# Expert weights loaded in rows of 8 KB, with the mixers' buffers in halves of the same places

## The chip, the cores and the metric

One core of one Trainium2 chip. The time is that of one execution on the device, in microseconds (us): the median of 3 runs. The engines are TensorE (PE, with its weight loads as PEld), VectorE (DVE), ScalarE (ACT), GpSimd (POOL) and SyncE (SP); sixteen DMA engines move data between the memory of the chip and the core's own, and work beside them.

## What is computed

One layer of a hybrid decoder for 512 tokens of width 1024, in f32. Four token mixers share one input projection; a layer norm follows, then 32 experts of which each token uses four, then an embedding with a gate, and a second layer norm.

```python
u = x @ w_in                                   # columns of SSD, RWKV-7, GLA, mLSTM
mix = concat([ssd(u_a), rwkv7(u_b), gla(u_c), mlstm(u_d)]) @ w_out
x = layer_norm(alpha * x + mix)
top_val, top_idx = top_k(x @ router_w + router_b, 4)
gate = softmax(top_val)
# for each token t and each of its four experts e:
hg, hl = split(x[t] @ w_gu[e] + b_gu[e], 2)    # 1024 x 2048
hg = minimum(hg, 7.0); hl = clip(hl, -7.0, 7.0)
y = ((hl + 1.0) * hg * sigmoid(1.702 * hg)) @ w_down[e] + b_down[e]
ffn[t] += gate[t, e] * y
h = alpha * x + ffn
h = h + sigmoid(h @ ple_gate_w) * (p @ ple_proj)
out = layer_norm(h)
```

Each expert has 12 MB of weights, 384 MB in all, and all of them are read once.

## The kernel before

**Stages.** The mixers, the output projection, the first layer norm and the router run from 0 to about 402 us. The 32 experts run one after the other from there to about 1496 us, and the end (the gate of the embedding, the second norm, the stores) to 1576.

**One expert.** The experts are sorted by the number of their tokens (`listed`, L1147), so that 18 get three groups of 32 · 4 slots each and 14 get two; `TURN` mixes them, and the first two in turn are the experts 0 and 1 themselves. In the loop at the end, `up` (L1293) multiplies the tokens' columns with the gate and value weights, 8 steps of k in four column quarters for each group; `swiglu` follows on DVE and ACT; `turned` transposes with TensorE; `tokens` (L1279) transposes the next expert's gathered rows; `down` (L1308) makes the second product; `put` scales and adds the rows in memory (`accd`) with a scatter from POOL (L1327). `dispatch` with `picked` (L1091) finds tokens and gates of the expert two places ahead with small matmuls, and `load` (L1208) gathers the next expert's rows of x from memory (`x1d`) into one of two `xg` buffers. For the first expert, `ranked`, `gates` and three dispatches stand between its up and its down product, then the gather for expert 1, and `blocks` (L1362), which makes a table of slots that did not fit.

**The weights' ring.** An expert's weights are 24 pieces of 128 x 1024 numbers, 512 KB, a row of 4 KB for each of 128 partitions. They are loaded by SP into a ring of 32 places (`seq`, L876) and, in the first round, into 4 more (`pp`), in the order of use. Most places are tiles that the mixers used before: 14 of tag `rb`, 8 of `r2`, 8 of `r3`, 2 of `wr`. `ahead` loads the first 15 pieces during the output projection. `unit` (L1213) issues one load when the piece that held the place before is marked `used`, that is after its last matmul in program order; `pump` issues as many as are free. Each load waits on SP for the place, and for a load eight issues before it. From the third expert on, the number of the expert is read from the sorted list `eii` by SP (`values_load`, L1228) once for each expert, at its first load in program order. The scheduler that builds the kernel sets the order of instructions on an engine; from the first expert on, TensorE keeps program order.

**At expert 20** three pieces more are loaded, the tokens' embeddings and their projection (`embed`); at the end, eight pieces of the gate's weights.

**In the mixers** two things matter here. Tiles of tag `rb` are what the change moves: `G` (products of the RWKV chain), `Tt` and `AQ` (its triangular inverse), `rk`, `ep`, `kp` and others. The chain has eight chunks in order; in each, a copy of the product `WO` to `W` (L445) waits for TensorE and TensorE's next step waits for it. `pj` and `pt` are products of the input projection, which fill TensorE between the chain's steps.

Of the kernel before, what the change touches and what calls it, by code (L numbers as in the profile page):

```python
# [8 lines left out]
F32 = mybir.dt.float32  # L9
# [16 lines left out]

SLOTS = {"rb": 14, "xh": 8, "wr": 2, "wh": 2, "wl": 2, "zb": 4, "zc": 7, "yy": 2, "rc": 4, "rd": 6, "mc": 5, "md": 4}
BANKS = {"r": 2, "o": 1, "p": 2, "m": 3}
RING2 = 8
RING3, XG, AB = 8, 2, 2  # L30
NS = 3
# [4 lines left out]
GROUPS_OF = [NS if r < BIG else NS - 1 for r in range(32)]  # L36
OPT = {"conv": ("sx0",), "lnt": ("vv","va","aa","va"), "lov": ("zb",), "pl": (0,5,8,13,16,21), "pt": (), "em": 20, "wk": 6, "ml": 0, "hold": 0, "gm": (0,), "pe": 0, "order": "SABZDIgvLqmoM", "wm": (10,8,0), "bn": (), "ad": (), "rb": (2,0,3), "pf": {(0,1):15}, "ex": 4, "xq": 1, "aq": 1,  "ap": 2, "t1": (8,8), "pa": 1,  "op": ((2,1),(0,))}
EMPTY = 4096.0
# [88 lines left out]
def mixers(tc, nc, A, rbp, dram, mix, ctx, ident, ones, tri, x1d, accd, R, dbg):  # L127
# [7 lines left out]
    pg = mix.enter_context(tc.tile_pool(name="pg", bufs=1, space=PSUM))  # L135

    def tl(tag, shape, name, dtype=F32):
        return {"rb": rbp, "zb": wz, "zc": wz, "rd": wz, "wr": wrp, "yy": wq, "rc": wq, "mc": wq}.get(tag, wk).tile(shape, dtype, name=name, tag=tag, bufs=SLOTS[tag])

# [141 lines left out]
    def rwkv():  # L281
# [596 lines left out]
    room = {**SLOTS, "r2": RING2, "r3": RING3, "pp": NT}  # L878

    def raw(look=False):  # L880

        n = R["n"]
        if n < len(seq) + OPT["ex"]:
            tag = (seq[:-2] + ["pp"] * OPT["ex"] + seq[-2:])[n]
        else:
            tag = seq[(n - OPT["ex"]) % len(seq)]
        if look:
            return tag, R["at"].get(tag, 0) % room[tag]
        R["n"] += 1
        R["at"][tag] = R["at"].get(tag, 0) + 1  # L890
        return R["pools"][tag].tile([128, D], F32, name="w", tag=tag, bufs=room[tag])

    def ahead(n):

        for _ in range(n):
            R["taken"].append(raw(look=True))
            w = raw()
            sy.dma_start(w, A["we"][0, len(R["pre"])])
            R["pre"].append(w)
# [159 lines left out]
def moe(ctx, tc, nc, A, ident, rbp, R, x1d, accd, ovt, ove, out, dbg):  # L1059
# [3 lines left out]
    xg = [xp.tile([128, D], F32, name=f"xg{i}", tag=f"xg{i}") for i in range(XG)]  # L1063
    g.memset(xg[0], 0.0)
    ep = ctx.enter_context(tc.tile_pool(name="ep", bufs=1))
# [58 lines left out]
    def gateweights():  # L1124

        for k in range(KT):
            w = ring[len(srcs) - KT + k]
            pool, tag, n = [(R["pools"]["r3"], "r3", RING3), (R["pools"]["wr"], "wr", SLOTS["wr"])][k] if k < 2 else (rbp, "rb", SLOTS["rb"])
            hi, lo = (pool.tile([128, D], F32R, name=x, tag=tag, bufs=n) for x in ("wh", "wl"))
# [71 lines left out]
    def dispatch(e):  # L1201

        picked(e, onehots(e, dp), lambda i: R["aux"][:, i, e], 5, e > 0, True)

# [10 lines left out]
    def unit(tag_of, src):  # L1215
# [9 lines left out]
        if isinstance(src, tuple):  # L1225
            j, u = src
            if j not in place:
                place[j] = nc.values_load(eii[0:1, TURN[j]:TURN[j] + 1], engines=[mybir.EngineType.SP], min_val=0, max_val=E - 1)  # L1228
            sy.dma_start(w[:, None], A["we"][bass.ds(place[j], 1), u].rearrange("o p n -> p o n"))
        else:  # L1230
            sy.dma_start(w, src)
        waits[tag, n] = len(ring)
# [4 lines left out]
    for e in range(E):  # L1237
        if e == OPT["em"]:
            srcs += [A["pT"], A["pproj"][0], A["pproj"][1]]
        srcs += [A["we"][e, u] if e < 2 else (e, u) for u in range(24)]  # L1240
    srcs += [A["pgw"][k] for k in range(KT)]
    base = lambda e: 24 * e + (3 if e >= OPT["em"] else 0)
    npre = len(R["pre"])
# [49 lines left out]
    def up(p, e, xT, g_, ks, last):  # L1293
        for k in ks:
            for c in range(4):
                w = ring[base(e) + 2 * k + c // 2][:, 512 * (c % 2):512 * (c % 2) + 512]
                ordered(pe.matmul(p[32 * c:32 * c + 32], xT[:, k, g_:32 * GROUPS_OF[TURN[e]]:GROUPS_OF[TURN[e]]], w,  # L1297
                                  start=False, stop=(k == KT - 1), tile_position=(0, 32 * c)))
            if last:
                used(base(e) + 2 * k)  # L1300
                used(base(e) + 2 * k + 1)

    def down(p, e, hT, ks, last):
        m = None
        for k in ks:
            for c in range(4):
                w = ring[base(e) + 16 + k][:, 256 * c:256 * c + 256]
# [38 lines left out]
    def embed(i, tag):  # L1346

        at = base(OPT["em"]) - 3
        pT, *pw = ring[at:at + 3]
        ppt.append(tp.tile([128, D], F32, name=f"pp{i}", tag="pp", bufs=NT))  # L1350
        tk = slice(128 * i, 128 * i + 128)
        for h in range(2):
            p = bank(tag, "emb")
            n = slice(512 * h, 512 * h + 512)
            for k in range(2):
                ordered(pe.matmul(p, pT[:, 512 * k:512 * k + 512][:, tk], pw[k][:, n], start=(k == 0), stop=(k == 1)))
            s.activation(ppt[i][:, n], p, AF.Copy)
        if i == NT - 1:
            for i in range(3):
                used(at + i)  # L1360
# [37 lines left out]
    def overflow(then):  # L1398
        with tc.tile_pool(name="ov", bufs=1) as ov:
            n = nc.values_load(tot[0:1, 0:1], min_val=0, max_val=24)  # L1400
            with tc.For_i(0, n, 1) as j:
# [24 lines left out]
                v.tensor_add(d[:, 3:4], d[:, 2:3], d[:, 3:4])  # L1426
                v.tensor_add(d[:, 3:4], d[:, 3:4], d[:, 4:5])
                def big(name):
                    return ring2.tile([128, D], F32, name=name, tag="r2", bufs=RING2)

# [16 lines left out]
                def product(ps, xT, units, view, o):  # L1447
                    for k in range(KT):
                        wt = big("wt")
                        sy.dma_start(wt[:, None], A["we"][bass.ds(e, 1), units[k]].rearrange("o p n -> p o n"))  # L1450
                        for i in range(2):
# [35 lines left out]
    with tc.issue_after(ix0), tc.issue_after(ld0):  # L1487
        g.dma_start(accd, x1d)
        for t in xg[1:]:
            g.memset(t, 0.0)  # L1490
        listed()
    for j in range(E):
# [30 lines left out]
        hT.extend(turned(act[:ns - 1], ["h"] * (ns - 1)))  # L1523
        if more and j:
            nxt = tokens(j + 1)
        hT.extend(turned(act[ns - 1:], ["h"]))
        pd = []
        for g_ in range(ns):
            pd.append(opened(j, "dn", 2048, 256))
            down(pd[g_], j, hT[g_], range(3), g_ == ns - 1)  # L1530
        for k in range(3, KT):
            for g_ in range(ns):
                down(pd[g_], j, hT[g_], [k], g_ == ns - 1)
        if j == OPT["em"]:
            embed(3, "gu")
        if more and not j:
            nxt = tokens(j + 1)
        for g_ in range(ns):
# [7 lines left out]
    def transposed(src):  # L1546

        hi, lo = (r3.tile([128, KT, 128], F32R, name="h" + x, tag="r3", bufs=RING3) for x in "hl")
        for h in range(2):
# [19 lines left out]
    def finish():  # L1569
        hs = []  # L1570
        for i in range(NT):
            hs.append(ring2.tile([128, D], F32, name=f"h{i}", tag="r2", bufs=RING2))
            for n in (slice(0, 512), slice(512, D)):
# [52 lines left out]
def _lay_out(inp, experts=True):  # L1626
# [45 lines left out]
    bg = a["exp_b_gu"][0].reshape(E, 2, 4, 256).transpose(0, 2, 1, 3).reshape(E, 2 * D)  # L1672
    r["bias"] = np.concatenate([bg, a["exp_b_down"][0]], 1)
    if experts:
        gu = a["exp_w_gu"][0].reshape(E, KT, 128, 2, 2, 2, 256).transpose(0, 1, 4, 2, 5, 3, 6).reshape(E, 16, 128, D)
        r["we"] = np.concatenate([gu, a["exp_w_down"][0].reshape(E, KT, 128, D)], 1)
    r["pT"] = a["p"][0, 0].T.reshape(2, 128, T).transpose(1, 0, 2).reshape(128, 2 * T)
    r["pproj"] = a["ple_proj"][0].reshape(2, 128, D)
    r["pgw"] = a["ple_gate_w"][0].reshape(KT, 128, D)
    return {k: np.ascontiguousarray(v) for k, v in r.items()}  # L1680
# [23 lines left out]
```

## Time and profile before

| | |
|---|---|
| median of 3 runs | 1579.39 us (1577.28 to 1581.19) |
| the profiled execution | 1578.24 us, of it the span from first to last instruction 1576.4 |
| TensorE busy | 1462.9 us (93%), weight loads 776.0 |
| VectorE, ScalarE, GpSimd busy | 522.9, 301.7, 218.2 us |
| moved by DMA | 466.13 MB, mean 296 GB/s |
| granted TensorE clock | 0.961 in the mean |

The profile is of one execution on the core. An engine counts as busy while it has an instruction, also when that instruction holds on for data. A share of the DMA engines is that of sixteen; it can be a little over 1, since packets of two queues overlap in the records. A number of microseconds after "<-" in a view is idle time and what ended it.

### The profile page before, as it was taken

What the parts mean: (1) busy time and instruction counts of PE and PEld (TensorE: products, weight loads), DVE (VectorE), ACT (ScalarE), POOL (GpSimd) and SP (SyncE); (2) the same over time, 40 slices, a digit from 0 to 9 for tenths busy, and PEclk for the clock granted to TensorE, in tenths of its full rate; (3) what the DMA queues carried; (4) which work ended last, traced back from release to release, by engine and by line L of the source; (5) the groups of instructions that cost most, each with busy time, mean ns of one, the idle gap of its engine ahead of it and who ended that gap; (6) DMA issues with size and microseconds to landing.
All of it is one profiled execution on the core that took longest, in us unless ns stands there. A gap on an engine that the chain in (4) does not pass through costs nothing. (4 is left out here: it accounts for less than half of the span.)

```text
span 1576.4 us, 36036 instructions
## 1 busy us (share of the span) xinstructions
PE 1462.9 (93%) x14672; PEld 776.0 (49%) x14672; DVE 522.9 (33%) x1597; ACT 301.7 (19%) x632; POOL 218.2 (14%) x222
## 2 busy tenths in 40 slices
PE   9989999997799999999999999999999998999985
PEld 5769879886244433443334333334434343334364
DVE  5688875668521112111121111111121111111155
ACT  4343523523011111110111110101111110111120
POOL 1011211003011211211111111111111211111100
PEclk9899999997899999999999999999999999999998
DMA  4222311654979999999999999999999999999931
GB/s 165 61 67 64 113 44 52 235 224 159 346 275 366 360 387 393 380 390 379 381 384 382 369 380 376 383 382 378 335 389 388 379 387 373 390 380 392 390 104 42
DMA packets 148012, 466.13 MB, mean 296 GB/s; under 512 B 27121, under 2 KB 36162, under 8 KB 147810
## 3 DMA queue, kind: packets, MB, share of 16 engines
q1 hardware_dynamic: 131666, 442.08, 74.2%
q0 software_dynamic: 14992, 18.90, 5.8%
q8 instruction: 117, 1.92, 0.5%
q10 hardware_dynamic: 1184, 2.80, 0.5%
q14 instruction: 53, 0.43, 0.1%
HBM read 452.08 MB, written 18.43 MB: 298 GB/s over the span
## 5 line engine op out<-in xcount | busy, mean ns | idle before, releaser
L1297 PE MATMUL gu<-w,x 128*32 128x512 f32 x5248 | 627.4, 596 | 22.7 <-DMA w<-in_we_dram 21.7
L1297 PEld LDWEIGHTS gu<-w,x 128*32 128x32 f32 x5248 | 189.1, 119 | 442.6 <-issue 292.8
L1316 DVE TENSOR_SCALAR a<-gu 128x256 f32<-128x256 f32 x82 | 34.8, 425 | 895.8 <-PE gu L1297 895.8
L1308 PE MATMUL dn<-w,h 128*32 128x256 f32 x5248 | 304.0, 387 | 0.6 <-issue 0.6
L1308 PEld LDWEIGHTS dn<-w,h 128*32 128x32 f32 x5248 | 160.4, 112 | 121.0 <-issue 8.7
L1327 POOL DMA_INDIRECT accd<-y,ixs x82 | 128.0, 1561 | 357.9 <-ACT y L1326 330.2
L1317 ACT ACTIVATE c<-a 128x256 f32<-128x256 f32 x82 | 34.2, 417 | 631.7 <-DVE a L1316 630.1
L1208 POOL DMA_INDIRECT xg<-x1d,ixt x32 | 32.8, 1025 | 585.2 <-PE tr L1279 524.1
L1326 ACT ACTIVATE y<-dn,gate 128x256 f32<-128x256 f32 x82 | 36.7, 473 | 273.2 <-PE dn L1308 273.2
L1279 PE MATMUL tr<-ident,xg 96*128 96x96 f32 (+1 forms) x256 | 31.6, 251 | 31.3 <-ACT h L1267 18.1
L1279 PEld LDWEIGHTS tr<-ident,xg 96*128 96x128 f32 (+1 forms) x256 | 22.6, 142 | 42.3 <-ACT h L1267 24.8
L158 DVE TENSOR_TENSOR wl<-w,wh 128x1024 fp32r<-128x1024 f32 x28 | 34.2, 1220 | 15.0 <-ACT wh L157 14.9
L1320 DVE TENSOR_TENSOR b<-b,c 128x256 f32<-128x256 f32 x82 | 34.9, 425 | 5.4
L1264 PE MATMUL tr<-ident,b 128*128 128x128 f32 x164 | 32.3, 298 | 4.7 <-DVE b L1320 1.6
L1319 DVE SCALAR_TENSOR_TENSOR b<-b,a 128x256 f32<-128x256 f32 x82 | 34.5, 421 | 1.8
L157 ACT ACTIVATE wh<-w 128x1024 fp32r<-128x1024 f32 x28 | 29.5, 1053 | 25.6 <-PE pj L144 17.4
L1280 ACT ACTIVATE x<-tr 128x384 f32<-128x384 f32 (+1 forms) x64 | 27.7, 443 | 34.2 <-PE tr L1279 33.2
L1318 DVE TENSOR_SCALAR b<-gu 128x256 f32<-128x256 f32 x82 | 34.0, 415 | 0.0
L1267 ACT ACTIVATE h<-tr 128x256 f32<-128x256 f32 x82 | 29.4, 381 | 15.1 <-PE tr L1264 12.2
L1089 DVE TENSOR_SCALAR pt<-iotas,rankm 128x384 bf16<-128x384 bf16 (+1 forms) x132 | 30.9, 295 | 0.0
L1289 PEld LDWEIGHTS <-sel 96*32 96x32 bf16 x656 | 17.8, 98 | 21.7 <-issue 9.9
L1596 PE MATMUL gu<-wh,hh 128*128 128x512 f32 (+1 forms) x72 | 27.6, 387 | 0.3 <-ACT hh L1554 0.3
(650 smaller groups left out, 1683.5 us busy)
## 6 DMA issues: line engine op xcount, KB each, us to landing
w<-in_we_dram SPq DMA_DIRECT2D x768, 512.0 KB
w<-in_wA_dram SPq DMA_DIRECT2D x18, 512.0 KB
w<-in_wT_dram SPq DMA_DIRECT2D x10, 512.0 KB
wo<-in_wO_dram SPq DMA_DIRECT2D x8, 512.0 KB
w<-in_pgw_dram SPq DMA_DIRECT2D x8, 512.0 KB
x<-in_xT_dram SPq DMA_DIRECT2D x4, 512.0 KB
xt<-in_xt_dram SPq DMA_DIRECT2D x4, 512.0 KB
x1d<-xt ACTq DMA_DIRECT2D x4, 512.0 KB
```

What stands on the lines that cost most here:

```text
L158: v.tensor_sub(wl, w, wh.bitcast(F32))
L1208: return g.indirect_dma_start(out=xg[TURN.index(e) % XG][0:n], out_offset=None, in_=x1d, in_offset=bass.IndirectOffsetOnAxis(ap=ixt[0:n, e ...
L1279: ordered(pe.transpose(p[:, n * k:n * k + n], xg[j % XG][0:n, c:c + 128], ident[0:n, 0:n]))
L1297: ordered(pe.matmul(p[32 * c:32 * c + 32], xT[:, k, g_:32 * GROUPS_OF[TURN[e]]:GROUPS_OF[TURN[e]]], w, start=False, stop=(k == KT - 1), ti ...
L1308: m = ordered(pe.matmul(p[32 * c:32 * c + 32, 0:256], hT[:, k % 2, 32 * (k // 2):32 * (k // 2) + 32], w, start=False, stop=(k == KT - 1), ...
L1316: v.tensor_scalar(a, p[:, 0:256], 7.0, None, op0=ALU.min)
L1317: s.activation(c, a, AF.Sigmoid, scale=1.702)
L1318: v.tensor_scalar(b, p[:, 256:512], 7.0, -7.0, op0=ALU.min, op1=ALU.max)
L1319: v.scalar_tensor_tensor(b, b, 1.0, a, op0=ALU.add, op1=ALU.mult)
L1320: v.tensor_mul(b, b, c)
L1326: last = s.activation(y, p[:, 0:256], AF.Copy, scale=gate[:, r, s_:s_ + 1]).ins
L1327: x = g.indirect_dma_start(out=accq, out_offset=bass.IndirectOffsetOnAxis(ap=ixs[:, r, s_:s_ + 1], axis=0), in_=y, in_offset=None, compute ...
```

## The change

Two consecutive pieces of an expert become one of 128 x 2048 numbers, 1 MB, a row of 8 KB for each partition; the weights lie in memory so. The ring has 16 places of 1 MB, and 2 more in the first round: the bytes are the same. Five of the places are new tiles `pair`, whose halves the mixers' tiles use (the table `HALF`), several one after the other in the same half: `G1` and `mq` after `rk`, `G2` after `sgw`, `G3` after `aa`, `Tt0` and `mk` after `ep`, and so on. `AQ` is written over `Lx`. The places of `wr` and `rb` (three of the sixteen) are still two tiles, and are loaded by two loads of 4 KB rows. A place is free again when both its halves are used. 6 places are loaded during the output projection, 6 MB where 7.5 MB were.

The read of the sorted list is put behind the load ahead of it. `first` finds and gathers the tokens of expert 1 too. The first expert's three dispatches stand behind the first three k of each group's down product, `blocks` behind the down product. Both `xg` buffers are cleared at the start. At the end the gate's weights and h take halves of the new tiles; that is left out here.

```diff
-SLOTS = {"rb": 14, ...
+SLOTS = {"rb": 4, ...
-RING2 = 8
-RING3, XG, AB = 8, 2, 2
+RING2 = 4
+RING3, XG, AB = 4, 2, 2
+PAIRS = 5
+HALF = {"sgw": 0, "aa": 1, "gg": 2, "rk": 3, "rr": 4, "ep": 5, "em": 6, "kp": 7, "AR0": 8, "AR1": 9, "G1": 3, "G2": 0,
+        "G3": 1, "rv": 6, "Tt0": 5, "Tt1": 7, "mq": 3, "mk": 5, "z_mo": 0}
...
+        if name in HALF:
+            n = HALF[name]
+            t = R["pairs"][n // 2][:, D * (n % 2):D * (n % 2) + D]
...
-        AQ = tl("rb", [128, 32, 32], "AQ")
+        AQ = Lx
...
-    seq = ["rb"] * 7 + ["r2"] * RING2 + ["rb"] * (SLOTS["rb"] - 9) + ["wr"] * 2 + ["r3"] * RING3 + ["rb"] * 2
+    seq = [3, 4] + ["r2"] * RING2 + [0, 1, 2] + ["wr"] + ["r3"] * RING3 + ["rb"] * 2
...
+    def loaded(w, src):
+
+        if isinstance(w, list):
+            for h in range(src.shape[-1] // D):
+                x = sy.dma_start(w[h], src[:, D * h:D * h + D])
+        else:
+            x = sy.dma_start(w[:, 0:src.shape[-1]], src)
+        return x.ins
...
         m, x = picked(0, onehots(0, dp), lambda i: R["auxi"][:, i], 2, True, False)
-        return m.ins, x.ins, load(0)
+        l = load(0)
+        with tc.issue_after(x.ins), tc.issue_after(l):
+            picked(1, onehots(1, dp), lambda i: R["auxi"][:, i], 2, True, False)
+            load(1)
+        return m.ins, x.ins, l
...
             if j not in place:
-                place[j] = nc.values_load(eii[0:1, TURN[j]:TURN[j] + 1], engines=[mybir.EngineType.SP], min_val=0, max_val=E - 1)
-            sy.dma_start(w[:, None], A["we"][bass.ds(place[j], 1), u].rearrange("o p n -> p o n"))
+                with tc.issue_after(state["load"]):
+                    place[j] = nc.values_load(eii[0:1, TURN[j]:TURN[j] + 1], engines=[mybir.EngineType.SP], min_val=0, max_val=E - 1)
+            src = A["we"][bass.ds(place[j], 1), u].rearrange("o p n -> p (o n)")
+        state["load"] = R["loaded"](w, src)
...
             if last:
-                used(base(e) + 2 * k)
-                used(base(e) + 2 * k + 1)
+                used(base(e) + k)
...
-            if last:
-                used(base(e) + 16 + k)
+            if last and k % 2:
+                used(base(e) + 8 + k // 2)
...
             ranked(nc, R, bank("tr", "tr"), marks, ordered)
             gates()
-            for r_ in TURN[:3]:
-                dispatch(r_)
-                if r_ == TURN[1]:
-                    load(r_)
-            tot, row = blocks()
...
             down(pd[g_], j, hT[g_], range(3), g_ == ns - 1)
+            if j == 0:
+                dispatch(TURN[g_])
...
-        if more and not j:
-            nxt = tokens(j + 1)
+        if j == 0:
+            tot, row = blocks()
```

**On SP, from the last loads of the first two experts on.** `w` and `pair_...` are places of the ring, `eii` is the sorted list, `otot`, `otab`, `oei` and `orow` belong to the table of `blocks`. Before:

```order
L1228 TENSOR_LOAD eii
L1228 ISA x2
L1231 DMA w<-in_we_dram 128x1024 x2
...
L1229 ISA
L1229 DMA w<-in_we_dram 128x1024
...
L1400 TENSOR_LOAD otot
L1400 ISA x2
L1392 DMA ovt<-otab 128x34
L1393 DMA ove<-oei 128x1
L1395 DMA orow<-ove 1x128
```

and after:

```order
L914 DMA w<-in_we_dram 128x2048 x4
L1264 TENSOR_LOAD eii
L1264 ISA x2
...
L914 DMA pair_108<-in_we_dram 128x2048
L1440 TENSOR_LOAD otot
L1440 ISA x2
...
L1432 DMA ovt<-otab 128x34
L1433 DMA ove<-oei 128x1
...
L914 DMA w<-in_we_dram 128x2048
L1435 DMA orow<-ove 1x128
```

Before, all thirty reads of the list stand among the last static loads; after, one stands ahead of each expert's first load. The table's transfers stood in one piece behind four loads, and now have loads between them.

**On TensorE, from the end of `ranked` to the first expert's down product.** `tr` is the bank for small products and transposes, `pt` the slots' one-hot rows, `b` the result of `swiglu`, `dn` the down product. Before:

```order
L1047 MATMUL tr<-marks,onb 128x32
L1100 LDWEIGHTS pt
L1100 MATMUL tr<-aux,pt 128x5
...
L1105 MATMUL tr<-aux,pt 96x2
L1264 MATMUL tr<-ident,b 128x128 x6
L1289 LDWEIGHTS sel
L1289 MATMUL dn<-bias,sel 32x256
...
L1308 MATMUL dn<-w,h 32x256 x12
```

and after:

```order
L1073 MATMUL tr<-marks,onb 128x32
L1305 MATMUL tr<-ident,b 128x128 x4
L1320 MATMUL tr<-ident,xg_3776 128x96 x8
L1305 MATMUL tr<-ident,b 128x128 x2
L1330 LDWEIGHTS sel
L1330 MATMUL dn<-bias,sel 32x256
...
L1348 MATMUL dn<-pair_109,h 32x256 x8
L1348 MATMUL dn<-w,h 32x256 x4
L1127 LDWEIGHTS pt
L1127 MATMUL tr<-aux,pt 128x5
```

The 36 products of five columns and 8 of two that stood ahead of the turns are now behind parts of the down product, and the transposes of expert 1's tokens stand ahead of it.

**On TensorE, in the mixers, from the last projection product ahead of the RWKV chain's `Q` to its first `WO`.** `Z` and `Q` make the inverse of a chunk, `G` is a chunk's product. Before:

```order
L144 MATMUL pt<-wl,x1h 128x256 x2
L144 MATMUL Q<-AQ,G_450 32x32 x8
L144 MATMUL Q<-AQ,G_451 32x32 x8
...
L144 MATMUL Z<-Tt_673,AQ 32x32 x16
L144 MATMUL Q<-AQ,G_452 32x32 x8
L144 MATMUL Q<-AQ,G_453 32x32 x8
...
L144 MATMUL WO<-VU,G_450 128x64 x4
```

and after:

```order
L155 MATMUL pj<-x2h,wl 128x512
L155 MATMUL Q<-Lx,G_445 32x32 x8
L155 MATMUL Q<-Lx,pair_108 32x32 x8
...
L155 MATMUL Z<-pair_109,Lx 32x32 x16
L155 MATMUL Q<-Lx,pair_107 32x32 x16
...
L155 MATMUL WO<-VU,G_445 128x64 x4
```

The chain's `Q` stands behind 325 `pj` and 288 `pt` products where it stood behind 288 and 156; between the first and the last `WO` product there are 96 `pj` and 192 `pt` where there were 144 and 289.

## Rows read from the trace of the kernel before

**Rows 1.** Busy time by stage: us, engines (count), PEclk, DMA share, GB/s

```profile
516.00:705.00 189.00, 184.07 (x2294) 76.46 (x2286) 31.92 (x126) 24.00 (x60) 29.69 (x22) 0.97 1.04 384
705.00:1484.00 779.00, 738.14 (x8362) 299.82 (x8356) 116.23 (x450) 90.85 (x222) 112.84 (x80) 1.00 1.03 380
```

**Rows 2.** What SP's queue waited for: total us, times, longest

```profile
SPq L1229 <- DMA w<-in_we_dram: 564.7, 624, 5.8
...
SPq L1229 <- PE gu L1297: 50.1, 97, 5.7
...
SPq L1395 <- DMA ove<-oei: 6.8, 1, 6.8
```

**Rows 3.** The same view, TensorE's weight loads (PEld)

```profile
PEld gu L1297 <- DMA w<-in_we_dram: 129.1, 162, 1.9
```

**Rows 4.** DMA view, 409 to 1484: packets, MB, share; loads issued

```profile
q1 hardware_dynamic: 105816, 384.27, 93.0%
...
w<-in_we_dram SPq DMA_DIRECT2D x732, 512.0 KB
```

**Rows 5.** Timeline of PE: start, us, what, count; first and unhindered experts

```profile
404.64 22.76 PE L1297 MATMUL gu<-w,x 128*32 128x512 f32 x192
...
450.02 20.77 PE L1297 MATMUL gu<-w,x 128*32 128x512 f32 x192
...
485.49 20.77 PE L1297 MATMUL gu<-w,x 128*32 128x512 f32 x192
506.20 0.48 PE L1100 MATMUL tr<-aux,pt 128*128 128x5 bf16 x12
...
520.59 13.91 PE L1297 MATMUL gu<-w,x 128*32 128x512 f32 x128
...
545.34 20.78 PE L1297 MATMUL gu<-w,x 128*32 128x512 f32 x192
...
582.07 13.90 PE L1297 MATMUL gu<-w,x 128*32 128x512 f32 x128
```

**Rows 6.** DMA view, 740 to 745 us: loads alone

```profile
q1 hardware_dynamic: 549, 2.01, 99.2%
```

**Rows 7.** DMA view, 1094.6 to 1095.4: one packet of 8 KB

```profile
q14 instruction: 1, 0.01, 2.4%
```

**Rows 8.** DMA view, 1505.9 to 1507.1: accd read in 2 KB rows

```profile
q1 hardware_dynamic: 216, 0.40, 99.4%
```

**Rows 9.** Busy time around the first down product, as rows 1

```profile
435.00:440.00 5.00, 4.75 (x52) 2.23 (x54) 3.09 (x25) 1.04 (x3) 2.09 (x2) 0.56 0.60 168
440.00:445.00 5.00, 5.00 (x100) 2.70 (x96) 0.00 (x0) 0.00 (x0) 0.00 (x0) 1.00 0.07 19
445.00:450.00 5.00, 5.00 (x88) 2.80 (x84) 0.00 (x0) 2.16 (x5) 1.41 (x1) 1.00 0.54 130
```

**Rows 10.** Timeline of SP's DMA issues: start, us, count

```profile
426.59 2.66 SPq L1229 DMA_DIRECT2D w<-in_we_dram  x4
...
446.40 5.22 SPq L1229 DMA_DIRECT2D w<-in_we_dram  x8
```

**Rows 11.** The list reads: ns min/median/max, first and last start

```profile
L1228 SPq TENSOR_LOAD <-eii x30: 262/268/472, 403.6 to 424.8; - x30
```

**Rows 12.** Timeline of POOL: the gather for expert 0

```profile
394.00 1.20 POOL L1208 DMA_INDIRECT xg<-x1d,ixt  x1 [1.83 <-DVE key L1161]
```

**Rows 13.** Mixers: two projection products by group, the chunk copies by line

```profile
L144 PE MATMUL pj<-x1h,wh 128*128 128x512 f32 x36 | 12.8, 439 | 0.0
...
L144 PE MATMUL pt<-wl,x0h 128*128 128x256 f32 x40 | 8.6, 293 | 0.0
...
L445 DVE COPY W<-WO x8: 427/428/429, 158.7 to 281.8; 64x256 f32<-64x256 f32 x8
```

**Rows 14.** Timeline of DVE: the first two of those copies

```profile
158.68 0.43 DVE L445 COPY W<-WO 64x256 f32<-64x256 f32 x1
...
169.03 0.43 DVE L445 COPY W<-WO 64x256 f32<-64x256 f32 x1 [0.81 <-PE WO L144]
```

More of the change, by code (lines that the diff above doesn't have):

```diff
@@ L874, in wout @@
         return split(A["wO"][h, kq], [128, 2, 512], "wo", *tags)
-    seq = ["rb"] * 7 + ["r2"] * RING2 + ["rb"] * (SLOTS["rb"] - 9) + ["wr"] * 2 + ["r3"] * RING3 + ["rb"] * 2
-    room = {**SLOTS, "r2": RING2, "r3": RING3, "pp": NT}
+    seq = [3, 4] + ["r2"] * RING2 + [0, 1, 2] + ["wr"] + ["r3"] * RING3 + ["rb"] * 2
+    room = {**{i: 1 for i in range(PAIRS)}, "r2": RING2, "r3": RING3, "pp": NT // 2, "wr": 1, "rb": 2}
     def raw(look=False):
@@ L890, in raw @@
         R["at"][tag] = R["at"].get(tag, 0) + 1
-        return R["pools"][tag].tile([128, D], F32, name="w", tag=tag, bufs=room[tag])
+        if tag in ("wr", "rb"):
+            return [R["pools"][tag].tile([128, D], F32, name="w", tag=tag, bufs=SLOTS[tag]) for _ in range(2)]
+        if tag in range(PAIRS):
+            return R["pairs"][tag]
+        return R["pools"][tag].tile([128, 2 * D], F32, name="w", tag=tag, bufs=room[tag])
+    def loaded(w, src):
[5 more added lines that the diff above has]
+        return x.ins
+    R["loaded"] = loaded
     def ahead(n):
@@ L1063, in moe @@
     xg = [xp.tile([128, D], F32, name=f"xg{i}", tag=f"xg{i}") for i in range(XG)]
-    g.memset(xg[0], 0.0)
+    for t in xg:
+        g.memset(t, 0.0)
     ep = ctx.enter_context(tc.tile_pool(name="ep", bufs=1))
@@ L1126, in gateweights @@
         for k in range(KT):
-            w = ring[len(srcs) - KT + k]
-            pool, tag, n = [(R["pools"]["r3"], "r3", RING3), (R["pools"]["wr"], "wr", SLOTS["wr"])][k] if k < 2 else (rbp, "rb", SLOTS["rb"])
-            hi, lo = (pool.tile([128, D], F32R, name=x, tag=tag, bufs=n) for x in ("wh", "wl"))
+            w = part(len(srcs) - KT // 2 + k // 2, D * (k % 2), D)
+            if k in (0, KT - 2, KT - 1):
+                q = "rb" if k else "wr"
+                hi, lo = (R["pools"][q].tile([128, D], F32R, name=x, tag=q, bufs=SLOTS[q]) for x in ("wh", "wl"))
+            else:
+                t = rbp.tile([128, 2 * D], F32R, name="whl", tag="pair", bufs=PAIRS)
+                hi, lo = t[:, 0:D], t[:, D:2 * D]
             s.activation(hi, w, AF.Copy)
@@ L1238, in moe, with part @@
         if e == OPT["em"]:
[L1239 to L1242, printed above, removed]
+            srcs += [A["pT"], A["pproj"]]
+        srcs += [A["we"][e, u] if e < 2 else (e, u) for u in range(12)]
+    srcs += [A["pgw"][k] for k in range(KT // 2)]
+    base = lambda e: 12 * e + (2 if e >= OPT["em"] else 0)
+    def part(i, at, n):
+        w = ring[i]
+        return w[at // D][:, at % D:at % D + n] if isinstance(w, list) else w[:, at:at + n]
     npre = len(R["pre"])
@@ L1295, in up @@
             for c in range(4):
-                w = ring[base(e) + 2 * k + c // 2][:, 512 * (c % 2):512 * (c % 2) + 512]
+                w = part(base(e) + k, 512 * c, 512)
                 ordered(pe.matmul(p[32 * c:32 * c + 32], xT[:, k, g_:32 * GROUPS_OF[TURN[e]]:GROUPS_OF[TURN[e]]], w,
@@ L1346, in embed @@
     def embed(i, tag):
[L1348 to L1351, printed above, removed]
+        at = base(OPT["em"]) - 2
+        if i % 2 == 0:
+            t = tp.tile([128, 2 * D], F32, name=f"pp{i}", tag="pp", bufs=NT // 2)
+            ppt.extend((t[:, 0:D], t[:, D:2 * D]))
         for h in range(2):
@@ L1355, in embed @@
             for k in range(2):
-                ordered(pe.matmul(p, pT[:, 512 * k:512 * k + 512][:, tk], pw[k][:, n], start=(k == 0), stop=(k == 1)))
+                ordered(pe.matmul(p, part(at, 512 * k + 128 * i, 128), part(at + 1, D * k + 512 * h, 512), start=(k == 0), stop=(k == 1)))
             s.activation(ppt[i][:, n], p, AF.Copy)
         if i == NT - 1:
-            for i in range(3):
+            for i in range(2):
                 used(at + i)
@@ L1427, in overflow @@
                 v.tensor_add(d[:, 3:4], d[:, 3:4], d[:, 4:5])
+                half = {}
                 def big(name):
-                    return ring2.tile([128, D], F32, name=name, tag="r2", bufs=RING2)
+                    if name in half:
+                        return half.pop(name)[:, D:2 * D]
+                    t = ring2.tile([128, 2 * D], F32, name=name, tag="r2", bufs=RING2)
+                    if name in ("x", "act"):
+                        half[{"x": "xT", "act": "hT"}[name]] = t
+                    return t[:, 0:D]
                 x = big("x")
@@ L1523, in moe @@
         hT.extend(turned(act[:ns - 1], ["h"] * (ns - 1)))
-        if more and j:
+        if more:
             nxt = tokens(j + 1)
@@ L1546, in transposed @@
     def transposed(src):
-        hi, lo = (r3.tile([128, KT, 128], F32R, name="h" + x, tag="r3", bufs=RING3) for x in "hl")
+        t = r3.tile([128, 2, KT, 128], F32R, name="hhl", tag="r3", bufs=RING3)
+        hi, lo = t[:, 0], t[:, 1]
         for h in range(2):
```

32 lines of the change are left out of this document (18 added, 14 removed).

## Prediction

> **What bounds the kernel now.** I read the busy time by stage first, then what SP and TensorE wait for, then the DMA view of the expert stage, and last the first expert, instruction by instruction. In the stage table [rows 1] the reader is to compare the DMA share with TensorE's: from 516 us on the sixteen DMA engines are busy all the time (1.04 and 1.03) at 380 to 384 GB/s, while TensorE looks 95 to 97% busy. TensorE's share deceives. It holds instructions that are waiting for weights: the weight loads of the up product waited 129.1 us for a load to land [rows 3]. The pace that TensorE has when nothing holds it stands early in the stage [rows 5]: an expert with three groups of slots takes 485.49 to 520.59 (35.1 us) or 545.34 to 582.07 (36.7), one with two takes 520.59 to 545.34 (24.75). With 17 × 35.8 + 14 × 24.75 and 45.4 for the first expert, 31 more experts after 404.6 are over at about 1405 us (the embedding of expert 20 comes on top); the trace still loads weights at 1484 [rows 1]. So the transfers have some 65 to 80 us on TensorE. SP says the same: it waited 564.7 us in 624 places for an earlier load to land and 50.1 us for a place that TensorE still held [rows 2]. The stage is bounded by how fast packets go through sixteen engines: 732 loads of 512 KB, and all hardware-queue packets hold 93.0% of the engines' time from 409 to 1484 [rows 4]. **A change is worth what it takes from the packets' time or from the time in which the engines have none.**
>
> **Rows of 8 KB.** A load of 128 rows gives each engine eight packets of 4 KB. 732 loads are 5,856 packets an engine. In the ring 13 of 16 places become one load of 8 KB rows; three stay two loads of 4 KB rows. So 4,758 packets become 2,379. What does one 8 KB packet cost? Clean 4 KB packets: in five microseconds between two scatters, 2.01 MB took 99.2% of 80 engine-us [rows 6], which is 491 packets of 161.7 ns each, their completion packets in it. The nearest rows with another length are two. A single 8 KB packet, of instructions and not of weights, took 2.4% of 12.8 engine-us [rows 7]; the share is rounded to a tenth, so 301 to 314 ns, 10 to 22 ns under two of 4 KB, 24 to 52 us in all. Reading accd in rows of 2 KB, 0.40 MB took 99.4% of 19.2 engine-us [rows 8], 98 ns for each of 195; two of those are 34 ns dearer than one of 4 KB, and the same step once more would be 80 us, which TensorE would cut at 65 to 80. Its source and its place in the program are other ones. The bounds are 0 (the engine cuts a row at 4 KB anyway) and 52; a loss is not excluded where a long packet holds up a gather or scatter, and that is costed below. I take 11 ns, the low end of the nearest row, since half of the stage runs beside scatters, where a part of each packet's time is spent on something else: 2,379 × 11 ns = **−26.2 us**. All of it is on the path, since the engines have no free time after 446, and TensorE has 65 us to give before it would be the bound.
>
> The Trainium skill (DMA: Bandwidth & Descriptors, Why small descriptors are slow) gives some three cycles and 32 bytes of descriptor to each packet; as an estimate from that page's 850 MHz this is under 5 ns, and the term would be −11. The nearest row's 10 to 22 ns decides until a run shows other.
>
> **The first expert.** Before, three dispatches stand between its up and its down product, and SP reads thirty list entries in a row. Its period is 404.64 to 450.02, 45.4 us [rows 5]. After, only `ranked` is left in front of the turns; the dispatches stand behind the first three k of each group's down product, and expert 1's tokens are gathered before the stage. Worked out: its up product 22.8 us, what the next expert needs besides its up (35.5 − 20.8 = 14.7), two dispatches more than that one has (0.5 us for twelve picks in a row, and one more for the four-pick form and the switch: 1.6 together [rows 5]), and 0 to 2 for the ranks' wait: 39 to 41. TensorE then has the second expert's up 4 to 6 us earlier. Is that worth anything to the DMA engines? They stood still here, which is rare: 0.60, 0.07 and 0.54 of 435 to 450 [rows 9], 9 us lost. The ring was full: SP had issued 52 loads into 36 places by 429 [rows 10], sixteen of them places that the up product gave back; and it then stood behind the overflow table, whose last transfer alone cost 6.8 us [rows 2], until 446.40 [rows 10]. The places come free with the down product, which now starts earlier; the wait for the table stays, with two places' loads put between its parts. So of the 9 us I take half: **−4 us** (0 to −8). The list reads themselves, 268 ns thirty times with two register steps [rows 11], cost before 415 us loads that the full ring took back: nothing. Spread out, one entry per expert, each waits behind the load ahead of it on SP and for nothing else, since the list is then long written; behind it on SP stand only loads, eight are in flight, and half a microsecond is hidden by them. It is free until fewer than one load is in flight.
>
> **What the change adds.** The gather of expert 0's rows [rows 12] now alternates with 8 KB packets: 96 rows are six on an engine, each may wait 145 ns longer, **+1**. Larger places: expert 20's first embedding stands behind two whole megabytes, and the very last place is used 0.5 MB later (1.3 us at 402 GB/s, less the matmuls of its first half): **+2** together (0 to +4). The prefetch of 6 MB instead of 7.5 is 1.5 MB later, 4 us of transfers, but the ring is full at 429 in either case, so it ends in the same idle time: 0, and up to +4 if the ring does not fill. The two memsets in front and the earlier gather on the GpSimd queue are about 2 us, beside DVE and the gather of expert 0, which is issued at 394.00 [rows 12] when the memset of the second buffer would have followed: 0 to +1.
>
> **The mixers.** The halves move places, and with them TensorE's order in the RWKV chain. By the order, the chain's first Q product stands behind 37 more projection products of 512 columns and 132 more of 256, and between the first and the last WO product there are 48 and 97 fewer. At 439 and 293 ns [rows 13] the latter is 49.5 us of TensorE's work. Eight chunks ran from 158.7 to 281.8 [rows 13], 17.6 us for each step; 123 − 49.5 leaves 10.5 for each, just what the shortest step shown takes (158.68 to 169.03 [rows 14]). So the end of the chain, and with it the start of the experts, stays where it is if every step is as short as the shortest. I take **+3** (−8 to +12): each microsecond here moves the end one to one.
>
> **Sum.** −26.2 − 4 + 1 + 2 + 3 = −24.2. The profiled execution took 1578.24 us (span 1576.4); it is 0.07% under the median of 1579.39, so to the median I add 1.15: 1578.24 − 24.2 + 1.15 = **1555.2**, told as 1555.
>
> **Rivals.**
> *No gain from longer rows.* The engines cut a row at 4 KB, or the time is bound by bytes at the memory. For it: with scatters in it the stage moves 380 GB/s [rows 1] and not 402, so part of a packet's time is not the engine's own. Against it: the dearer 2 KB rows and the single 8 KB packet [rows 7, 8], both of which say that a packet has a price of its own. Then only the other terms are left, +2: 1581, or 1578 without the mixers' term.
> *The chain of the mixers is stretched (slower).* Nothing is left between the chunks' products for TensorE to do, so a step that takes longer than 10.5 us holds it, and the experts start later. For it: a step averaged 17.6 before, and a copy waits for the WO product even in a short one [rows 14]. Against it: what made most steps long is just the projection work that is no longer between them. At 14.4 us a step (7 × 3.9 = 27) the whole gain is gone, at 16 us it is 1579.4 − 27.2 + 38.5 = 1591. It decides from about 15 us a step.
> *The number of loads, not of packets, is what costs.* If each load's end held an engine back, half of the ends would go, and the loads would run until TensorE bounds: 65 to 75 us less, about 1510. Against it: with 512 KB a load the engines are 99.2% busy with packets [rows 6]; there is no gap to close. The Trainium skill (DMA: Bandwidth & Descriptors, Bandwidth) asks for at least 1 MiB a transfer and lists 341 GB/s for 1 MB; by the trace eight loads of half that already give 402.
>
> **How the numbers follow.** Chances: the forecast 0.74, no gain from rows 0.12, the stretched chain 0.09, the count of loads 0.05. The forecast's own spread is 1538 (16 ns a packet and 6 from the first expert, no price for the mixers) to 1576 (5 ns and +10 for the mixers). The range for 8 in 10 reaches up over half of the first rival: 1538 to 1581. A measurement of this kernel can tell 0.3% (4.7 us) from no change. Faster by more: most of the forecast (0.70), the third rival and a little of the first: 0.77. Within: 0.04 of the forecast and 0.08 of the first: 0.12. Slower: 0.11.
>
> **What would show it.** Right: from 450 to 1484 the hardware queue has some 45,000 packets fewer, a share of the engines' time that stays at 1.0, and a rate of 390 GB/s or more in stretches that had 380; 415 or more in a microsecond without scatters. The first up product of expert 1 starts 39 to 42 us after that of expert 0. The first weight product of the experts starts within 8 us of 404.64. Wrong: the rate stays near 380 (first rival); the chunk copies are further apart than 11 us and the experts start after 415 (second); TensorE no longer waits for weights (third); or the engines stand still longer than 9 us around the first down product, because places of a megabyte come free later than halves did.

## The result, and the profile after

| | before | after |
|---|---|---|
| median | 1578.34 us (1576.9 to 1581.19, 4 runs) | 1557.46 us (1555.2 to 1560.23, 4 runs) |
| span of the profiled execution | 1576.4 | 1553.4 |
| granted TensorE clock, mean | 0.961 | 0.957 |

The ratio is 0.9859 (95% interval 0.9842 to 0.9876), a gain of 20 to 25 us. Forecast were 1555 us and a gain of 24.2. The sum was close; several of its terms were not, and their errors had opposite signs. They are the lesson.

The stage of the experts, by the table of stages (us, busy time of PE, PEld, DVE, ACT, POOL with counts, granted clock, DMA share, GB/s):

```profile
516.00:705.00 189.00, 184.13 (x2250) 74.90 (x2246) 31.81 (x126) 22.89 (x57) 32.70 (x24) 0.97 1.03 392
705.00:1462.00 757.00, 705.13 (x8312) 284.39 (x8301) 117.03 (x452) 90.76 (x221) 108.42 (x77) 0.98 1.01 387
```

Against [rows 1] the rate went from 384 to 392 and from 380 to 387 GB/s, and the share fell a little, from 1.04 and 1.03 to 1.03 and 1.01. TensorE still waits for weights, less than in [rows 3], so the transfers are still the bound. What TensorE's weight loads waited for:

```profile
PEld gu L1338 <- DMA w<-in_we_dram: 68.0, 65, 2.9
PEld gu L1338 <- DMA pair<-in_we_dram: 24.7, 25, 3.1
```

The DMA view from 409 to 1462 us (queue: packets, MB, share of sixteen engines; then the loads issued, with the time from issue to landing):

```profile
q1 hardware_dynamic: 62889, 384.89, 92.4%
q0 software_dynamic: 14434, 16.19, 7.7%
...
w<-in_we_dram SPq DMA_DIRECT2D x184, 1024.0 KB, 18.6
pair<-in_we_dram SPq DMA_DIRECT2D x114, 1024.0 KB, 18.8
w<-in_we_dram SPq DMA_DIRECT2D x134, 512.0 KB, 17.3
```

62,889 packets stand where [rows 4] had 105,816, for the same bytes: 42,927 fewer, of the 45,000 forecast. The first expert, in TensorE's timeline (start, us, what, count), as [rows 5]:

```profile
403.24 6.98 PE L1338 MATMUL gu<-pair,x 128*32 128x512 f32 x48
...
442.66 15.63 PE L1338 MATMUL gu<-w,x 128*32 128x512 f32 x144
```

The second expert follows 39.4 us after the first, instead of 45.4. The first starts 1.4 us earlier, which says little: in ten of the kernels below, whose mixers are the same, it starts between 401.9 and 406.6. The engines' pause around the first down product, as [rows 9] (the busy columns are as in the first table):

```profile
430.00:435.00 5.00, 5.00 (x106) 2.67 (x99) 4.67 (x30) 0.04 (x1) 0.00 (x0) 1.00 0.39 159
435.00:440.00 5.00, 5.00 (x100) 3.25 (x104) 2.03 (x15) 0.00 (x0) 0.97 (x1) 1.00 0.81 282
440.00:445.00 5.00, 5.00 (x80) 2.38 (x72) 0.00 (x0) 1.34 (x3) 1.63 (x1) 1.00 1.20 194
445.00:450.00 5.00, 5.00 (x52) 1.59 (x48) 0.00 (x0) 0.00 (x0) 0.00 (x0) 1.00 0.86 187
```

Free time is (0.61 + 0.19 + 0.14) × 5 = 4.7 us, where 9 were. But from 440 to 450 the engines count as busy and move 190 GB/s; that is new. What SP waited for (total us, times, longest):

```profile
SPq L914 <- DMA w<-in_we_dram: 360.2, 209, 4.5
...
SPq L914 <- PE gu L1338: 72.1, 62, 16.7
...
SPq L912 <- PE emb L1396: 16.5, 2, 16.2
...
SPq L1435 <- DMA ove<-oei: 7.1, 1, 7.1
```

The longest, 16.7 us, lies ahead of the first expert: the ring is full and TensorE has not given a place back. The surprise is the wait of 16.2 us for the embedding of expert 20. It shows in the stages as a pause of the engines:

```profile
1090.00:1095.00 5.00, 4.59 (x45) 2.54 (x47) 0.85 (x6) 2.62 (x6) 1.01 (x1) 1.00 0.73 265
1095.00:1100.00 5.00, 5.00 (x100) 2.88 (x96) 0.00 (x0) 0.00 (x0) 0.00 (x0) 1.00 0.35 139
1100.00:1105.00 5.00, 5.00 (x40) 2.02 (x29) 0.00 (x0) 1.73 (x4) 3.11 (x2) 1.00 0.27 52
```

(0.27 + 0.65 + 0.73) × 5 = 8.3 us without transfers.

### The profile page after: what moved, and what is told of

The parts are those of the page before. It is cut to its first block, busy times and chain, and to the rows that moved or that the text cites. A ratio compares the mean times of both kernels' runs of the same rounds, so it can differ in the third digit from the quotient of the medians.

```text
span 1553.4 us, 34857 instructions
## 1 busy us (share of the span) xinstructions
PE 1428.9 (92%) x14671; PEld 756.1 (49%) x14672; DVE 521.9 (34%) x1601; ACT 301.3 (19%) x632; POOL 223.4 (14%) x222
## 5 line engine op out<-in xcount | busy, mean ns | idle before, releaser
L1338 PE MATMUL gu<-w,x 128*32 128x512 f32 x3568 | 412.4, 597 | 24.9 <-DMA w<-in_we_dram 24.5
L1338 PEld LDWEIGHTS gu<-w,x 128*32 128x32 f32 x3568 | 119.4, 119 | 298.9 <-issue 227.1
L1348 PE MATMUL dn<-w,h 128*32 128x256 f32 x3664 | 218.7, 392 | 0.0
L1338 PE MATMUL gu<-pair,x 128*32 128x512 f32 x1680 | 197.5, 602 | 8.2 <-DMA pair<-in_we_dram 8.0
L1348 PEld LDWEIGHTS dn<-w,h 128*32 128x32 f32 x3664 | 113.7, 113 | 85.8 <-issue 8.8
L1338 PEld LDWEIGHTS gu<-pair,x 128*32 128x32 f32 x1680 | 55.7, 120 | 134.9 <-issue 107.4
L1348 PE MATMUL dn<-pair,h 128*32 128x256 f32 x1584 | 96.6, 394 | 1.0 <-DMA pair<-in_we_dram 1.0
L1348 PEld LDWEIGHTS dn<-pair,h 128*32 128x32 f32 x1584 | 48.8, 114 | 38.7 <-issue 4.9
```

## Rows or loads: four kernels that move the same bytes

The change made the rows longer and the loads larger at once. Three kernels and the changed one fill a table with one thing altered at a time. Ring, prefetch and TensorE's work are those of the changed kernel in all four.

**Loads of 512 KB, rows of 4 KB**, as before the change. The weights lie in memory in pieces of 128 x 1024 again:

```diff
+        if len(src.shape) == 3:
+            n, q = src.shape[-1], D // src.shape[-1]
...
+                for h in range(2):
+                    x = sy.dma_start(w[:, D * h:D * h + D].rearrange("p (q n) -> p q n", n=n), src[:, q * h:q * h + q])
```

> The changed kernel with its order, ring and prefetch untouched, but each place of 1 MB filled by two loads of 512 KB with rows of 4 KB, as before the change. Theory 'packets' (a packet has a price of its own, about 11 ns, whatever load it belongs to): the 2,379 packets saved on each engine are back, +24 to +26 us, so about 1582 us; the rate of the expert stage falls from 387 back to about 380 GB/s. Theory 'loads' (the end of each load holds the engines back): the same, +24. Theory 'order' (the gain came from the first expert and the mixers): within 5 us of 1557.

Measured: 1574.97 us, 0.9983 of before (0.9971 to 0.9996). 17.5 us of the gain are gone, and some 3 are left (0.6 to 4.6 by the interval), which are not the weights' transfers.

**Loads of 1 MB, rows of 4 KB.**

```diff
+        if len(src.shape) == 3:
+            n, q = src.shape[-1], D // src.shape[-1]
...
+                x = sy.dma_start(w.rearrange("p (q n) -> p q n", n=n), src)
```

> Loads of 1 MB as in the changed kernel, but each made of two pieces of 128 rows of 4 KB: number of loads as after, packets as before. Theory 'packets': about 1582 us, as with 512 KB loads, and 40,000 packets more in the expert stage. Theory 'loads': 1557, as after. Theory 'order': 1557.

Measured: 1567.88 us, 0.9932 of before (0.9916 to 0.9949): between the two theories. Neither is enough alone.

**Loads of 512 KB, rows of 8 KB.** A load of half the bytes with whole rows has 64 partitions. The first form took the lower and the upper half:

```diff
-            x = sy.dma_start(w[:, 0:src.shape[-1]], src)
+            for o in (0, 64):
+                x = sy.dma_start(w[o:o + 64, 0:src.shape[-1]], src[o:o + 64])
```

> Loads of 512 KB of 64 partitions each with rows of 8 KB: number of loads as before, packets as after. Theory 'packets': 1557 us, plus 0 to 3 because eight loads in flight are now 4 MB and not 8. Theory 'loads': about 1582.

Measured: 2255.83 us (2219 to 2286), 660 to 730 us over the changed kernel, which no theory had. The engines are busy and slow; the DMA view from 1000 to 1005 us, a stretch that no other queue shares:

```profile
DMA packets 204, 1.12 MB, mean 224 GB/s; under 512 B 33, under 2 KB 33, under 8 KB 102
...
q1 hardware_dynamic: 204, 1.12, 104.5%
```

102 of the packets are of 8 KB and 69 of 4 KB (the three places that are still two tiles). 1.12 MB in 83.6 engine-us are 610 ns for every 8 KB, twice the 307 of [rows 7]. The same with the even and then the odd partitions:

```diff
-            x = sy.dma_start(w[:, 0:src.shape[-1]], src)
+            for o in (0, 1):
+                x = sy.dma_start(w[o::2, 0:src.shape[-1]], src[o::2])
```

> As the loads of 64 partitions with 8 KB rows, but the two loads of a place take the even and the odd partitions, not the lower and the upper half. Theory 'ports' (a load into 64 neighbouring partitions goes through half of the ways into the core's memory): the loss of 700 us is gone, and what is left against the changed kernel is the price of 366 loads more: 1557 to 1566. Theory 'fewer rows' (a load of 64 rows, four on an engine, is slow in any place): 2100 to 2300 again.

Measured: 1563.0 us, 0.9905 of before (0.9887 to 0.9922). The loss is gone: it belongs to 64 neighbouring partitions, not to 64 rows. That is what the theory 'ports' had; the ports themselves no run here shows. The table of medians:

| | rows of 4 KB | rows of 8 KB | gain by rows |
|---|---|---|---|
| loads of 512 KB | 1575.0 | 1563.0 | 12.0 |
| loads of 1 MB | 1567.9 | 1557.5 | 10.4 |
| gain by loads | 7.1 | 5.5 | |

So **10 to 12 us come from longer rows and 5.5 to 7 from fewer loads**. With eight loads in flight, loads of 1 MB also have twice the bytes in flight; no run tells the two apart, so "fewer loads" stands for both.

Why not 26 from the rows? The view that is cleanest for this is a long stretch in which the transfers bound every kernel, 820 to 1060 us. The hardware queue there (packets, MB, share), of the kernel before:

```profile
q1 hardware_dynamic: 23856, 86.87, 94.5%
```

of the kernel with loads of 512 KB and rows of 4 KB:

```profile
q1 hardware_dynamic: 23848, 86.85, 94.7%
```

with 1 MB and 4 KB:

```profile
q1 hardware_dynamic: 23170, 88.33, 94.9%
```

with 512 KB and 8 KB, on even and odd partitions:

```profile
q1 hardware_dynamic: 15649, 88.79, 93.9%
```

and of the changed kernel:

```profile
q1 hardware_dynamic: 14684, 89.74, 94.1%
```

The share of 240 us of sixteen engines, divided by the MB, is the price of a MB in engine-us: 41.8, 41.9, 41.3, 40.6 and 40.3. The first two agree, so nothing else of the change touches the price. Rows of 8 KB take off 1.0 (1 MB loads) to 1.3 (512 KB). A MB has 122 packets of 8 KB, of which 13 in 16, 99, replace a pair: 10 to 13 ns for each pair. **The price of 11 ns was right.** What was wrong is that a nanosecond of packet time is a nanosecond of time: the packets' records overlap, and some of what the hardware queue gave up was overlap. In this stretch the shares of all queues add up to 1.03 before and 1.02 after. Counted packet by packet from 450 us to the last weights, what is under way beyond sixteen packets at once comes to 36 us of the sixteen engines' time before, 35 with 1 MB and 4 KB, and 26 after. The stretch's rate comes nearer: 88.33 to 89.74 MB is 1.6%, of some 1050 us 17; and measured were 10 to 12. It flatters too, however: from 86.85 to 89.74 MB, for rows and loads together, it would be 3.3% or 34 us, and measured were 17.5. From 450 to 1440 us, almost the whole stage, the hardware queue of the kernel with 512 KB and 4 KB and that of the changed kernel show

```profile
q1 hardware_dynamic: 98186, 357.55, 93.8%
```

```profile
q1 hardware_dynamic: 59460, 365.30, 92.8%
```

which is 2.2% or some 22 us. What takes the rest is open; from 450 us on and outside 1085 to 1125 the engines' free time is about the same, 4.4 us of the sixteen engines' time before and 4.6 after.

**Rows of 2 KB in loads of 1 MB**, in all sixteen places (the piece's `n` is 512):

> Loads of 1 MB, rows of 2 KB in all places: 11,712 packets on an engine for the 366 MB of the expert stage, against 3,477. Theory 'packets' with a fixed 11 ns each: +91 us, about 1648. If the price of a packet is that of the 2 KB rows read from accd (98 ns each against 161.7 for 4 KB, so 34 ns): about +200 to +280, about 1800. Theory 'loads' or 'order': 1557.

Measured: 1615.32 us, 1.023 of before (1.021 to 1.0249). Against 1 MB with 4 KB it is 47.4 us more for 5,856 packets more on an engine: 8.1 ns of time each. Its queue in the same stretch:

```profile
q1 hardware_dynamic: 42539, 84.00, 96.9%
```

44.3 engine-us for a MB, 3.0 more than with 4 KB, for 244 packets more: 12.5 ns of packet time each. From 2 to 8 KB a packet's own price is thus about the same, and the 34 ns read from [rows 8] belong to reading accd at that place, not to the row's length. The Trainium skill (DMA: Bandwidth & Descriptors, Why small descriptors are slow) gives each packet some three cycles and each pair of descriptors 32 bytes, under 5 ns by its 850 MHz as an estimate; the engines' records show 10 to 13 and the kernels' times 4 to 8 (10.4 us over 2,379 pairs, 47.4 over 5,856). The measurement decides: its order is right, its size low against the records.

## The first expert: dispatches or list

**Dispatches back** between the first expert's up and down product:

```diff
             gates()
+            for r_ in TURN[:3]:
+                dispatch(r_)
...
-            if j == 0:
-                dispatch(TURN[g_])
```

> The changed kernel with the first expert's three dispatches back between its up and its down product; the tokens of expert 1 are still gathered before the stage. Theory 'dispatch' (the 6 us of the first expert come from these): the second expert starts 45 us after the first instead of 40, and the whole takes 4 to 6 us more, about 1562. Theory 'list' (they come from the list reads, which are off SP's way): second expert at 40 us, 1557.

Measured: 1562.92 us, 0.9899 of before (0.9882 to 0.9915), 5.5 more than the changed kernel. Its first up product and the next expert's, in TensorE's timeline:

```profile
404.89 5.79 PE L1338 MATMUL gu<-pair,x 128*32 128x512 f32 x48
...
449.07 11.33 PE L1338 MATMUL gu<-w,x 128*32 128x512 f32 x104
```

44.2 us from one to the next, where the changed kernel has 39.4.

**The list read in one row** again:

```diff
-                with tc.issue_after(state["load"]):
+                if True:
                     place[j] = nc.values_load(eii[0:1, TURN[j]:TURN[j] + 1], engines=[mybir.EngineType.SP], min_val=0, max_val=E - 1)
```

> The changed kernel with the thirty reads of the sorted list in one row again, ahead of the loads. Theory 'dispatch': the ring fills a little later and is full all the same: 1557 to 1559, the second expert still 40 us after the first. Theory 'list': the second expert 44 to 46 us after the first, about 1562.

Measured: 1556.35 us, 0.9858 of before (0.9841 to 0.9875), no difference. The next expert follows after 39.6 us:

```profile
404.25 7.12 PE L1338 MATMUL gu<-pair,x 128*32 128x512 f32 x48
...
443.84 15.63 PE L1338 MATMUL gu<-w,x 128*32 128x512 f32 x144
```

So this part of the gain is the dispatches, and the half of the change that concerns the list is worth nothing. SP issues its next loads at 413.2 us instead of 407.7, behind the reads, and by 426 its issues stand a microsecond behind those of the changed kernel, as TensorE does.

## The pauses that are left

**The embedding first.** All four parts of it ahead of expert 20's up product:

```diff
         if j == OPT["em"]:
-            embed(0, "dn")
+            for i_ in range(NT):
+                embed(i_, "dn")
```

with the other three calls left out.

> The changed kernel with all four parts of the embedding in front of expert 20's up product, so that their two places are free some 30 us earlier. If the 16 us in which SP stands for these places cost what the engines' idle time there shows (about 8.5 us from 1090 to 1105, against 3 before the change): SP's wait for the embedding under 3 us, 4 to 8 us less, about 1551. If TensorE, 15 us later in its up product, then holds up the ring in its turn: 1557.

Measured: 1553.75 us (1550.66 to 1554.64), 0.9843 of before (0.9827 to 0.986). SP's wait for the embedding (total us, times, longest) is next to nothing, and the stretch in which the engines had paused is full:

```profile
SPq L912 <- PE emb L1396: 0.3, 1, 0.3
```

```profile
1090.00:1095.00 5.00, 5.00 (x50) 1.27 (x43) 1.49 (x4) 0.42 (x1) 0.00 (x0) 1.00 1.00 391
1095.00:1100.00 5.00, 4.23 (x52) 2.58 (x52) 2.94 (x16) 1.97 (x5) 1.01 (x1) 0.82 0.97 362
1100.00:1105.00 5.00, 5.00 (x84) 2.68 (x80) 0.00 (x0) 0.00 (x0) 0.00 (x0) 0.83 0.99 327
```

Expert 20's up product starts some 10 us later, behind the three parts that now stand ahead of it; they are gone from behind it, and expert 21 starts 1.9 us later than in the changed kernel (1107.50 against 1105.63). The gain over the changed kernel, 3.7 us by the medians, is near the noise of two sets of four runs.

**The overflow table's row read late**, so that SP does not stand 7.1 us for it:

```diff
-        sy.dma_start(row, ove.rearrange("p o -> o p"))
...
+        if j == 4:
+            with tc.issue_after(state["load"]):
+                sy.dma_start(row, ove.rearrange("p o -> o p"))
```

> The changed kernel with the read of the overflow table's row, for which SP stands 7.1 us behind the write of it, put off to the end of the fifth expert. Theory 'SP' (the three loads behind it were free to go): the engines' low rate from 440 to 450 (about 190 GB/s) goes up to 300 or more, and 1 to 3 us less, about 1555. Theory 'ring' (the places were full anyway): no change, 1557.

Measured: 1559.08 us, 0.9884 of before (0.9857 to 0.9912): no gain. Two of the three loads that stood behind it go out 1 to 4 us earlier, and the rate stays low:

```profile
440.00:445.00 5.00, 5.00 (x92) 2.76 (x88) 0.00 (x0) 1.34 (x3) 1.48 (x1) 1.00 1.25 266
445.00:450.00 5.00, 5.00 (x52) 1.60 (x48) 0.00 (x0) 0.00 (x0) 0.15 (x1) 1.00 0.86 162
```

2.14 MB in these ten microseconds instead of 1.91. What slows the engines there, with megabytes in their queues, is not settled: the first scatter, the table's small writes and a gather fall together in it. **Both edits together:**

> The embedding in front of expert 20 and the row's read put off, together. If both are worth what each alone is: about 1552 (1553.75 with the embedding alone, less 1 to 3).

Measured: 1554.37 us (1553.77 to 1556.25), 0.9855 of before (0.983 to 0.9881): the embedding's gain and nothing more.

**The copy into accd late.** GpSimd's copy of x1d, in rows of 64 KB, waits for the first expert's transposes (with the embedding first):

```diff
+        state["m"] = m
...
-        g.dma_start(accd, x1d)
+        behind(g.dma_start(accd, x1d).ins, state["m"].ins)
```

> The changed kernel with the embedding in front of expert 20 (1553.75 us so far) and the copy of x1d into accd, in rows of 64 KB, put behind the first expert's transposes instead of right behind its gather. TensorE waits 7.9 us for that gather, whose 96 rows share the engines with 8 KB packets and stand ahead of the copy on GpSimd's queue. Theory 'copy' (the copy's long packets hold the last rows of the gather or its end): TensorE's wait falls to 4 to 6 us and the experts start 2 to 4 us earlier, about 1551. Theory 'queue of loads' (the gather waits for the megabytes of weights already in the rings): no change, 1554.

Measured: 1554.63 us, 0.9853 of before (0.9836 to 0.9869). TensorE's wait for the gather did not get shorter (total us, times, longest):

```profile
PE tr L1321 <- DMA xg<-x1d,ixt: 8.2, 1, 8.2
```

It was 7.9. The gather does not wait for the copy behind it; whether it waits for the loads already in the engines' queues, or takes this long by itself, was not tried.

Of the eleven kernels the three with the embedding first are the fastest, 1553.75 to 1554.63 us, 3 to 4 below the changed kernel's median and 2 to 3 below the kernel that only reads the list at once. Their intervals against before overlap those of the changed kernel. The cleanest pair, however, is the kernel with both edits against the one with the row's read alone, run together: they differ in the embedding only, and all four times of the first (1553.77 to 1556.25) are below all four of the second (1558.03 to 1562.16), 4.7 us by the medians. So the embedding in front is worth some 4 us.

## Why the prediction was right, point by point

- **The bound** was read rightly: the transfers set the pace after the change too, and TensorE's slack was not used up but at expert 20 (below). The sign "390 GB/s or more" came out at 387 to 392; from 1115 to 1120 us, with nothing beside them, the loads ran at 421.
- **Rows of 8 KB, −26.2.** The price of a packet was right in the engines' time (11 against 10 to 13 ns); the step that failed is "all of it is on the path". Rows brought 10 to 12 us. It was made up in part by fewer loads, 5.5 to 7 us, which the prediction had only as a rival that excluded the other, with a chance of 0.05, because the engines were 99.2% busy with packets [rows 6]. But that busy time is not the data's alone: by the five prices of a MB, 0.3 to 0.6 engine-us go with the size of the loads. What in it this is, a load's end or something else, the records do not show; a full engine does not mean that only the data costs. Together the weights' transfers gave 17.5 us.
- **The first expert, −4.** Right, with 39.4 us inside the 39 to 41 worked out. Undoing it costs 5.5, inside the 0 to 8 given. That the list is worth nothing was right as well.
- **The gather +1 and the mixers +3.** By the spread given above, the experts' start did not move. The chain's copies, in the view of that line (ns min/median/max, first and last start):

```profile
L456 DVE COPY W<-WO x8: 427/427/428, 174.0 to 284.9; 64x256 f32<-64x256 f32 x8
```

  The last copy is 3.1 us later than in [rows 13], as taken; later parts of the stage give that back. The way there was wrong: the chain starts 15 us later, not some 50, and a step takes 15.8 us, not 10.5. By the forecast's own sum steps of that length would have lost the whole gain; that the two errors cancelled is luck. I had priced the projection products by the mean duration of one (439 and 293 ns), but products overlap on TensorE: 40 of them have a busy time of 8.6 us together [rows 13], 215 ns each, and those of 512 columns 356. With these, 48 and 97 products are 38 us and not 49.5. That leaves 12.2 us a step; what makes it 15.8 is open. The rival that rested on it, a stretched chain, was therefore less likely than I gave it.
- **Larger places, +2.** The size fits, the way does not. The piece with the embeddings, 512 KB, now holds a place of a megabyte; it and its neighbour are given back, as before, only after the fourth part of the embedding, and SP stood there for 16.2 us in front of all later loads. Before, the longest such wait was 2.2 us, and the engines' pause some 3 us:

```profile
SPq L1229 <- PE emb L1356: 2.8, 3, 2.2
```

```profile
1115.00:1120.00 5.00, 5.00 (x82) 2.58 (x75) 0.00 (x0) 0.91 (x2) 0.43 (x1) 1.00 0.41 133
```

  The kernel with loads of 512 KB and rows of 4 KB has the larger places too, at the rate of before:

```profile
SPq L914 <- PE emb L1405: 10.7, 2, 10.4
```

```profile
1110.00:1115.00 5.00, 5.00 (x93) 2.69 (x86) 0.00 (x0) 0.42 (x1) 0.00 (x0) 1.00 0.41 135
1115.00:1120.00 5.00, 4.86 (x28) 1.92 (x32) 0.00 (x0) 1.68 (x4) 3.11 (x2) 1.00 0.49 84
```

  Its pause is 5.5 us. So about half of the growth from 3 to 8.3 us stands there with the places alone; the other half is seen only where the transfers are faster. Removing the whole pause gave 3.7 to 4.7 us, of which only a part is the change's, so +2 (0 to +4) is not refuted. The step that failed is that I priced the arrival of a larger piece and not its release.
- **Sum.** −17.5 for the transfers, with the second half of the larger pause in it, and the 3.4 us that the kernel with 512 KB and 4 KB keeps (1578.34 − 1574.97): 20.9, against 24.2. The forecast had −26.2 for the transfers and +2 for all the rest; measured are −17.5 and −3.4. That the sum came out within 4 us is thus in part luck: the transfers brought 9 us less, the rest 5 us more.

## What to carry to other kernels

Where transfers are the bound, price a packet from two rows of different length, but do not count all of it as time: here 2,379 pairs at 10 to 13 ns are 24 to 31 us of each engine's time, and 10 to 12 us were gained. The rate of the whole stage comes nearer than that of a short stretch (22 and 34 us, where 17.5 were measured). Change row length and number of loads apart, since both count: here they gave 10 to 12 and 5.5 to 7 us. When places of a ring get larger, look for the one whose content is used last: its release, not its arrival, stops the queue.

## What was not expected of the hardware

With loads into 64 neighbouring partitions the core moved 224 GB/s between 1000 and 1005 us with the engines fully busy, 610 ns for every 8 KB, and 235 GB/s from 820 to 1060, where the changed kernel moved 391; with every second partition the same number of rows, packets and loads took 1563 us for the kernel instead of 2256. The Trainium skill (DMA: Bandwidth & Descriptors, Rules for kernel authors) says of two transfers to disjoint halves of the partitions that they serialize on the same engines and advises one of 128. The advice holds here, but that they share the engines is not what costs: the even and the odd partitions share them too and ran at 387 GB/s from 820 to 1060, and the halves lost some 40% of the rate.
